# Where a chunk's output lies, in which order its loads are issued, and when two sets of weights are split

## The chip, the cores and the metric

The kernel runs on one core of a Trainium2 chip. Its engines work from queues of their own: TensorE (PE in the rows, PEld for its weight loads), VectorE (DVE), ScalarE (ACT), GpSimd (POOL) and SyncE (SP), which issues nearly all transfers. The metric is the device time of one execution in microseconds. Each engine takes its instructions strictly in the order of its queue, so an instruction that waits holds up all that stand behind it on that engine.

## The reference

One decoder layer on 1024 tokens of width 1024, all in f32. What matters here, cut:

```python
proj = jnp.einsum('bld,de->ble', h, w_in[i])
xs, z, bm, cm, dt_raw, glu, cgate = jnp.split(proj, SPLITS, axis=-1)
...
y = ssd_chunked(xh, dt, a, bm_c, cm_c)          # chunks of 128 tokens
y = y + d_skip * xh
yz = y * jax.nn.silu(z)
yz = yz * lax.rsqrt(jnp.mean(jnp.square(yz), axis=-1, keepdims=True) + RMS_EPS)
y_ssm = yz * ssm_norm_g[i]
...                                             # conformer group: y_conf
mix = jnp.concatenate([y_ssm, y_conf], axis=-1)
out = jnp.einsum('ble,ed->bld', mix, w_out[i]) + b_out[i]
h = layer_norm(DEEPNORM_ALPHA * h + out, ln1_g[i], ln1_b[i])
gate = jax.nn.sigmoid(jnp.einsum('bld,de->ble', h, w_ple_gate[i]))
ple = jnp.einsum('blq,qd->bld', p[i], w_ple_proj[i])
h = layer_norm(DEEPNORM_ALPHA * h + gate * ple, ln2_g[i], ln2_b[i])
```

## The kernel before, in words

Every large matrix product is made of three matmuls of rounded parts: an operand is split into an upper part (a cast on ScalarE) and a lower part (what is left, a subtraction on GpSimd or VectorE), by `split` (L128) or, for weights with a scale, in `out_weight` (L430). `out_weight` loads one slab of 128 rows of weights into `wor` (SP, L433) and leaves `woh` and `wol`.

The work has these stages. First come the embedding norm, the input projection of all 44 column blocks and two causal convolutions; results that later chunks need go to DRAM (`xbc_d`, `z_d`, `acs_d`, `ea_d`, `mix_d`). At about 545 us the last block, a `z_tile`, ends, and its result `zt` is stored to `z_d` (L398).

Then comes the loop over eight chunks of 128 tokens (L698 to L727). Chunk c does on PE, in this order (the order is pinned): `from_state` (L508, `yo`, not for chunk 0), the transposes `xtok` and `bps` of chunk c+1 (`prep`), part of the conformer half of the output projection (`conf_out`, `pso`), `inside` (L521, `yd`), more `pso`, `advance` (L536, `sp`, which moves the state on), `mean_square` of the chunk before (L557, `pr`) and more `pso`. Around it VectorE adds the skip to `yd` and writes the chunk's output `y` (L531); GpSimd multiplies it by silu(z), the tile `sz` that `z_load` brings back from `z_d` (L549); ScalarE squares it into the tile `ea` (L552); GpSimd folds the squares twice (L553, L554); `pr` takes their mean. The loads of chunk c+2 are `prep_load` (`xb` at L454, two `gt` at L459, whose exponentials ScalarE forms at L464), `state_decay` (`ea`, L472) and `z_load` (`sz`, L505). `xb` goes into the place of the chunk two before, which VectorE's `y` reads last.

`y` lives in a pool of two places (tag "y"). Just before the loop the same two places hold `zt` of the last two `z_tile`s and a raw weight tile, and the last `zt` leaves its place when its store has landed.

PE's `yd` and `sp` share three places of PSUM: the second `sp` of a chunk takes that of the first `yd`, which VectorE's `y` has to have read.

After the loop come two products. `out_proj(c)` (L605) multiplies the gated output, read back and split by `y_load` (L590), by the first eight slabs of `wout` (`ws`; slabs 0 to 2 are split inside the loop, 3 to 7 behind it), in four groups `pss` of twelve matmuls, each closed by VectorE's `r` (L616). The groups take turns in two places of PSUM, which `conf_out` uses too: the second group needs the last `ha` (L585) of `conf_out` to have read its place, the third needs the first `r`. In PE's queue the first ten matmuls of group one come first, then ten of group two, then the last two of each (those that read `wol` of slab 3), then groups three and four. `gate` (L630) then multiplies by `wgate` (`wg`, groups `psg`).

A scheduler places instructions on each queue by its own estimate of when each can run. `tc.keep_in_program_order(...)` exempts an instruction from that: it stays where the program has it. The lines that set it in the parts touched:

```python
def on_pe(ins):
    if pinned:
        tc.keep_in_program_order(ins)
...
nc.scalar.activation(out=h.bitcast(F32R), in_=raw, func=AF.Copy, scale=scale)
tc.keep_in_program_order(nc.vector.scalar_tensor_tensor(out=l.bitcast(F32R), ...))
```

Of the kernel before, what the change touches and what calls it, by code (L numbers as in the profile page):

```python
# [9 lines left out]
F32R = mybir.dt.float32r  # L10
AF = mybir.ActivationFunctionType
ALU = mybir.AluOpType
PSUM = bass.MemoryType.PSUM

P = 128
L = 1024
D = 1024
NK = 8
NT = 8
HEADS = 16  # L20
HD = 64
# [25 lines left out]
def tile_block(ctx: ExitStack, tc: tile.TileContext, x, pT, wple, win, wdt, wout, wgate, vec, rows, heads, out):  # L47
    nc = tc.nc
# [24 lines left out]
    z_d = tc.dram_tile([NT, P, NK, P], F32, name="z_d")  # L73
    acs_d = tc.dram_tile([P, P], F32, name="acs_d")
# [6 lines left out]
    def work(name, tag, n=L):  # L81
        return wk.tile([P, SIZE.get(tag, L)], F32, name=name, tag=tag, bufs=BUFS[tag])[:, 0:n]

    def slabs(a, n=NK):
        return a.rearrange("p (k l) -> p k l", k=n)
# [16 lines left out]
    def v(name, i=0, n=1):  # L102
        return vc[:, VEC[name] + i:VEC[name] + i + n]
# [21 lines left out]
    dec = const.tile([P, P], F32, name="dec")  # L125
    cdec = const.tile([P, P], F32, name="cdec")

    def split(src, h, l, leng):  # L128

        nc.scalar.copy(out=h.bitcast(F32R), in_=src)  # L130
        leng.tensor_tensor(out=l.bitcast(F32R), in0=src, in1=h, op=ALU.subtract)  # L131

    def three(ps, lh, ll, rh, rl, first, last):
        mm(ps, lhsT=ll, rhs=rh, start=first, stop=False)
# [22 lines left out]
    def area(name, tag):  # L157
        return regA.tile([P, L], F32, name=name, tag=tag, bufs={"W": 8, "E": 4, "M": 4}[tag])
# [268 lines left out]
    def bslot(name, tag):  # L427
        return regB.tile([P, D], F32, name=name, tag=tag)

    def out_weight(src, get, tag, last, scale=None, leng=nc.gpsimd):  # L430

        raw = area("wor", last) if last == "W" else work("wor", last) if last else get("wor", tag)
        nc.sync.dma_start(out=raw, in_=src)  # L433
        h, l = get("woh", tag), get("wol", tag)
        if scale is None:
            split(raw, h, l, leng)
        else:
            nc.scalar.activation(out=h.bitcast(F32R), in_=raw, func=AF.Copy, scale=scale)
            tc.keep_in_program_order(nc.vector.scalar_tensor_tensor(out=l.bitcast(F32R), in0=raw, scalar=scale, in1=h, op0=ALU.mult, op1=ALU.subtract))
        return h.bitcast(F32R), l.bitcast(F32R)  # L440

# [3 lines left out]
    def col(a, c, h, n=1):  # L445
        return a[:, c * HEADS + h:c * HEADS + h + n]

    def heads3(a):
        return a.rearrange("p (h d) -> p h d", d=HD)

    def prep_load(c):

        xb = slabs(work("xb", "xb", 12 * P), 12)
        nc.sync.dma_start(out=xb, in_=xbc_d[c])  # L454
        gg = []
        for g in range(2):
            gt = slabs(work("gt", "gt"))
            r0 = c * HEADS + g * 8
            nc.sync.dma_start(out=gt, in_=acs_d[r0:r0 + 8, :].unsqueeze(0).broadcast_to([P, 8, P]))  # L459
            gg.append(gt)  # L460

        for h in range(HEADS):
            sl = gg[h // 8][:, h % 8, :]
            nc.scalar.activation(out=sl, in_=sl, func=AF.Exp, bias=col(nacs, c, h))  # L464
        return xb, gg

    def state_decay(c):

        ea = slabs(work("ea", "u") if c == 0 else area("ea", "E"))
        for q in range(2):  # L470
            er = ea_d[c * HEADS:(c + 1) * HEADS, :].rearrange("(t q) l -> q t l", q=2)[q]
            nc.sync.dma_start(out=ea[q * HD:(q + 1) * HD], in_=er.unsqueeze(0).broadcast_to([HD, NK, P]))  # L472
        return ea

    def prep(c, xb, gg):

        def late(ins):

            if c < 2:
                tc.keep_in_program_order(ins)  # L480

        xdt = work("xdt", "xd")
        xt = pair("xtok")
        for t in range(NK):
            transpose(out=xt[:, t * P:(t + 1) * P], in_=xb[:, t, :], identity=ident)
        late(nc.vector.tensor_tensor(out=heads3(xdt), in0=heads3(xt), in1=col(dtok, c, 0, HEADS).unsqueeze(2).broadcast_to([P, HEADS, HD]), op=ALU.mult))
        xdd = (work("xdd", "u") if c == 0 else area("xdd", "E")) if c + 1 < NT else None
        for h in range(HEADS if c + 1 < NT else 0):
            nc.scalar.activation(out=xdd[:, h * HD:(h + 1) * HD], in_=xdt[:, h * HD:(h + 1) * HD], func=AF.Copy, scale=col(dec, c, h))
        bps = bbank("bps")  # L490
        for g in range(2):
            transpose(out=bps[:, g * P:(g + 1) * P], in_=xb[:, 8 + g, :], identity=ident)
            mm(bps[:, (2 + g) * P:(3 + g) * P], lhsT=xb[:, 8 + g, :], rhs=xb[:, 10 + g, :], start=True, stop=True)
        btok = wk.tile([P, 2 * P], F32, name="btok", tag="btok")
        nc.scalar.copy(out=btok, in_=bps[:, 0:2 * P])
        cbm = wk.tile([P, 2, P], F32, name="cbm", tag="cbm", bufs=1)
        late(nc.vector.tensor_tensor(out=cbm, in0=bps[:, 2 * P:4 * P].rearrange("p (g l) -> p g l", g=2),
                                     in1=tri.unsqueeze(1).broadcast_to([P, 2, P]), op=ALU.mult))
        for g in range(2):
            late(nc.vector.scalar_tensor_tensor(out=gg[g], in0=gg[g], scalar=1.0, in1=cbm[:, g:g + 1, :].broadcast_to([P, 8, P]), op0=ALU.min, op1=ALU.mult))  # L500
        return xb, gg, xdt, xdd, btok

    def z_load(c):
        sz = slabs(work("sz", "u") if c else area("sz", "W"))
        nc.sync.dma_start(out=sz, in_=z_d[c])  # L505
        return sz

    def from_state(c, xb, ea):  # L508

        for g in range(2):  # L510
            es = ea[:, g * 4:g * 4 + 4, :]
            yo = bank("yo")
            for t in range(4):
                j = g * 4 + t
                mm(yo[:, t * P:(t + 1) * P], lhsT=state[:, j * P:(j + 1) * P], rhs=xb[:, 10 + g, :], start=True, stop=True)
            nc.vector.tensor_tensor(out=es, in0=slabs(yo, 4), in1=es, op=ALU.mult)
        if c + 1 < NT:
            nc.gpsimd.tensor_tensor(out=heads3(state), in0=heads3(state),
                                    in1=col(cdec, c, 0, HEADS).unsqueeze(2).broadcast_to([P, HEADS, HD]), op=ALU.mult)
# [70 lines left out]
    def y_load(c):  # L590
        raw = slabs(work("yraw", "y"))
        nc.sync.dma_start(out=raw, in_=y_d[c])
        yH = slabs(work("yH", "xd"))

        split(raw, yH, raw, nc.vector if c < 2 else nc.gpsimd)
        return yH.bitcast(F32R), raw.bitcast(F32R)


# [83 lines left out]
    regs = [(bslot, "B1")] * 4 + [(bslot, "B2")] * 4  # L682
    conf = [conf_out(0, *mix_load(0))]
    wc = [out_weight(wout[NK + k], *regs[k], {3: "y", 7: "W"}.get(k)) for k in range(NK)]

    def turn(n):
        for _ in range(n):
            if next(conf[0], conf) is conf:
                conf.pop(0)
                next(conf[0])  # L690

    state = work("state", "st")
    szs = [z_load(0)]
    eas.append(state_decay(1))
    szs.append(z_load(1))
    ws = []
    sq = None
    for c in range(NT):  # L698
        xb, gg, xdt, xdd, btok = ready.pop(0)
        ea = eas.pop(0)  # L700
        y = slabs(work("y", "y"))
        pinned.append(True)
        if c:
            from_state(c, xb, ea)
            if c + 1 < NT:
                ready.append(prep(c + 1, *loaded))
            turn(5)
        for g in range(2):
            inside(c, g, y, xb, gg, ea, xdt)
        turn(3 if c else 2)  # L710
        if c + 1 < NT:
            conf.append(conf_out(c + 1, *mix_load(c + 1)))
        if c:
            turn(2)
        if c + 1 < NT:
            advance(c, xdd, btok)
        if c:
            mean_square(c - 1, sq)
        if c + 2 < NT:
            loaded = prep_load(c + 2)  # L720
            eas.append(state_decay(c + 2))
        sq = gated(c, y, ea, szs.pop(0))
        if c + 2 < NT:
            szs.append(z_load(c + 2))
        if c < 3:
            ws.append(out_weight(wout[c], area, "W", None, v("sng", c)))
        turn(6)  # L727
# [3 lines left out]
    pinned.clear()  # L731
    ys = []
    for k in range(3, NK):
        if k in (4, 6):
            ys.append(y_load(len(ys)))
        ws.append(out_weight(wout[k], area, "W" if k < 4 else "E" if k < 6 else "M", {4: None, 5: "u", 7: "u"}.get(k, "xb"), v("sng", k)))
    gb = []
    for i in range(4):
        r = work(f"gb{i}", "gt")
# [5 lines left out]
    for c in range(2):  # L745
        rs.append(out_proj(c, *ys.pop(0)))
        if c == 0:
            wg = [out_weight(wgate[k], *regs[k], "xb" if k % 4 == 3 else None, leng=nc.vector if k % 2 else nc.gpsimd) for k in range(NK)]
        ys.append(y_load(c + 2))
    for c in range(NT):  # L750
        if c + 2 < NT:
# [57 lines left out]
```

## Time and profile before

| | us |
|---|---|
| median of 3 runs (lowest, highest) | 895.61 (894.19, 896.59) |
| the profiled execution | 894.83 |
| its span | 893.1 |
| PE busy in the span | 863.2 (97%) |
| VectorE, ScalarE, GpSimd busy | 641.2, 389.1, 515.3 |

The span is the part of the execution that the profiler's instructions cover. PE is the engine that works nearly all the time: 29.9 us of the span are left in which it does not. Two stretches stand out in the page's 40 slices, where PE's granted clock shows 8 in place of 9. All times in the rows below count from the start of the span; in brackets stands how long the engine sat idle before a row and what ended that.

### The profile page before, as it was taken

The numbers are of one execution on the slowest core, as the hardware profiler recorded it, in microseconds if no ns is written. First come the engines' busy times: TensorE is split into PE (matmuls) and PEld (weight loads), VectorE is DVE, ScalarE is ACT, GpSimd is POOL, SyncE is SP. The second block draws the span as 40 slices with busy tenths as digits, with TensorE's granted clock in tenths as the row PEclk, the third lists the DMA queues.
The fourth block names the chain that finished last, engine by engine and source line by source line (L and its number), as shares of the span: only waits on it lengthen the run. The fifth ranks groups of instructions, "written<-read, shape, count | busy, mean of one in ns | idle before, by whom it ended". The sixth has DMA issues, their size and how long they took to land. (4 is left out here: it accounts for less than half of the span.)

```text
span 893.1 us, 10971 instructions
## 1 busy us (share of the span) xinstructions
PE 863.2 (97%) x4141; PEld 706.9 (79%) x4141; DVE 641.2 (72%) x739; ACT 389.1 (44%) x633; POOL 515.3 (58%) x297
## 2 busy tenths in 40 slices
PE   6989999999999999999999997999999799999996
PEld 4867888888888888888788885888888678888885
DVE  6968993799999989894403941676654796777765
ACT  4632336767333457553475735745453321111110
POOL 2559829999823299999572254766775362222111
PEclk9999999999999999999999998999999899999999
DMA  9702423121322314233241678799868812222212
GB/s 338 275 36 96 172 87 117 32 95 47 95 67 76 95 47 150 86 95 94 71 141 48 181 245 273 265 345 294 262 222 295 310 42 95 95 94 77 83 51 74
DMA packets 67716, 126.42 MB, mean 142 GB/s; under 512 B 4176, under 2 KB 41552, under 8 KB 67664
## 3 DMA queue, kind: packets, MB, share of 16 engines
q1 hardware_dynamic: 67664, 125.73, 42.1%
q8 instruction: 32, 0.52, 0.2%
q14 instruction: 20, 0.16, 0.1%
HBM read 89.93 MB, written 35.78 MB: 141 GB/s over the span
## 5 line engine op out<-in xcount | busy, mean ns | idle before, releaser
L57 PE MATMUL ps<-hL,wh 128*128 128x512 f32 x704 | 274.6, 391 | 1.1 <-DVE hL L190 1.1
L57 PE MATMUL ps<-hH,wl 128*128 128x512 f32 x704 | 274.2, 391 | 1.5 <-DVE hH L188 1.5
L57 PE MATMUL ps<-hH,wh 128*128 128x512 f32 x704 | 274.3, 390 | 0.0
L302 DVE SCALAR_TENSOR_TENSOR pc<-u,vc,pc 128x1024 f32<-128x1024 f32 x174 | 223.9, 1287 | 3.5
L297 POOL TENSOR_TENSOR acc<-acc,prod 128x1024 f32<-128x1024 f32 x60 | 146.4, 2440 | 17.9 <-ACT acc L293 15.0
L131 POOL TENSOR_TENSOR wl<-wraw,wh 128x1024 fp32r<-128x1024 f32 x44 | 110.7, 2515 | 77.1 <-PE ps L57 41.4
L57 PEld LDWEIGHTS ps<-hL,wh 128*128 128x128 f32 x704 | 132.2, 188 | 29.0 <-DVE hL L190 1.5
L57 PEld LDWEIGHTS ps<-hH,wl 128*128 128x128 f32 x704 | 131.8, 188 | 28.8 <-DVE hH L188 2.0
L57 PEld LDWEIGHTS ps<-hH,wh 128*128 128x128 f32 x704 | 132.2, 188 | 27.5 <-issue 0.2
L143 POOL TENSOR_SCALAR ve<-mv 128x1 f32<-128x1 f32 x23 | 15.8, 688 | 142.3 <-DVE mv L154 100.0
L296 ACT ACTIVATE prod<-u,vc 128x1024 f32<-128x1024 f32 x60 | 69.0, 1153 | 45.7 <-POOL acc L297 35.6
L130 ACT CAST wh<-wraw 128x1024 fp32r<-128x1024 f32 x44 | 46.2, 1051 | 67.0 <-DMA wraw<-in_win_dram 40.7
L643 ACT ACTIVATE gt<-psg 128x512 f32<-128x512 f32 (+1 forms) x17 | 9.7, 573 | 120.4 <-PE psg L57 120.4
L391 DVE SCALAR_TENSOR_TENSOR pc<-xin,vc,pc 128x512 f32<-128x512 f32 x72 | 53.7, 750 | 6.0 <-ACT pc L258 3.4
L57 PE MATMUL pss<-woh,yraw 128*128 128x512 f32 x128 | 51.3, 402 | 5.7 <-DVE r L616 5.7
L57 PE MATMUL pso<-woh,mL 128*128 128x512 f32 x128 | 53.6, 419 | 0.0
L57 PE MATMUL psg<-woh,hTL 128*128 128x512 f32 (+1 forms) x136 | 52.0, 383 | 0.0
L57 PE MATMUL psg<-woh,hTH 128*128 128x512 f32 (+1 forms) x136 | 52.0, 382 | 0.0
L616 DVE SCALAR_TENSOR_TENSOR r<-pss,rsm,r 128x512 f32<-128x512 f32 x32 | 23.8, 747 | 39.2 <-PE pss L57 32.7
L57 PE MATMUL psg<-wol,hTH 128*128 128x512 f32 (+1 forms) x136 | 51.5, 378 | 0.0
L57 PE MATMUL pss<-woh,yH 128*128 128x512 f32 x128 | 50.6, 396 | 0.0
L57 PE MATMUL pso<-wol,mH 128*128 128x512 f32 x128 | 50.6, 395 | 0.0
(184 smaller groups left out, 1460.7 us busy)
## 6 DMA issues: line engine op xcount, KB each, us to landing
wraw<-in_win_dram SPq DMA_DIRECT2D x44, 512.0 KB, 3.6
gt<-acs_d SPq DMA_DIRECT2D x16, 512.0 KB, 4.6
wor<-in_wout_dram SPq DMA_DIRECT2D x16, 512.0 KB, 5.6
xbc_d<-cacc SPq DMA_DIRECT2D x12, 512.0 KB, 3.4
xb<-xbc_d SPq DMA_DIRECT2D x8, 768.0 KB, 6.6
xt<-in_x_dram SPq DMA_DIRECT2D x8, 512.0 KB, 9.0
ple_d<-pl SPq DMA_DIRECT2D x8, 512.0 KB, 4.8
ha_d<-xt SPq DMA_DIRECT2D x8, 512.0 KB, 4.8
```

Of the source, the lines that this page charges most:

```text
L57: on_pe(nc.tensor.matmul(*args, **kw))
L130: nc.scalar.copy(out=h.bitcast(F32R), in_=src)
L131: leng.tensor_tensor(out=l.bitcast(F32R), in0=src, in1=h, op=ALU.subtract)
L143: eng.tensor_scalar(out=ve, in0=var, scalar1=EPS, scalar2=None, op0=ALU.add)
L296: nc.scalar.activation(out=pr, in_=u[:, i:i + L], func=AF.Copy, scale=v("ccw", j * KC + i))
L297: nc.gpsimd.tensor_tensor(out=acc, in0=acc, in1=pr, op=ALU.add)
L302: nc.vector.scalar_tensor_tensor(out=pc if i + 1 < KC else acc, in0=u[:, i:i + L], scalar=v("ccw", j * KC + i), in1=pc, op0=ALU.mult, op1= ...
L391: nc.vector.scalar_tensor_tensor(out=pc, in0=xin[:, o + j:o + j + 512], scalar=v("scw", i * 4 + j), in1=pc, op0=ALU.mult, op1=ALU.add)
L616: nc.vector.scalar_tensor_tensor(out=r[:, nn], in0=ps, scalar=rss[c][:, g:g + 1], in1=r[:, nn], op0=ALU.mult, op1=ALU.add)
L643: nc.scalar.activation(out=gt[:, nn], in_=ps, func=AF.Sigmoid)
```

## The change

The first chunk's `y` is put into the area "W" (the places of the input projection's `hH`, free after its last matmul). The loads of the loop's start are put in another order, and those of chunk 2 and the first `sz` are pinned in it (`behind`). Chunk 1's gated output is loaded and split behind all eight slabs of `wout`, its lower part on GpSimd in place of VectorE and pinned. The upper parts of scaled weights are pinned as well, and both parts of the gate weights.

```diff
@@ -125,10 +125,13 @@
     dec = const.tile([P, P], F32, name="dec")
     cdec = const.tile([P, P], F32, name="cdec")
 
-    def split(src, h, l, leng):
-
-        nc.scalar.copy(out=h.bitcast(F32R), in_=src)
-        leng.tensor_tensor(out=l.bitcast(F32R), in0=src, in1=h, op=ALU.subtract)
+    def split(src, h, l, leng, placed=False):
+
+        upper = nc.scalar.copy(out=h.bitcast(F32R), in_=src)
+        lower = leng.tensor_tensor(out=l.bitcast(F32R), in0=src, in1=h, op=ALU.subtract)
+        if placed:
+            tc.keep_in_program_order(upper)
+            tc.keep_in_program_order(lower)
 
     def three(ps, lh, ll, rh, rl, first, last):
         mm(ps, lhsT=ll, rhs=rh, start=first, stop=False)
@@ -427,15 +430,15 @@
     def bslot(name, tag):
         return regB.tile([P, D], F32, name=name, tag=tag)
 
-    def out_weight(src, get, tag, last, scale=None, leng=nc.gpsimd):
+    def out_weight(src, get, tag, last, scale=None, leng=nc.gpsimd, placed=False):
 
         raw = area("wor", last) if last == "W" else work("wor", last) if last else get("wor", tag)
         nc.sync.dma_start(out=raw, in_=src)
         h, l = get("woh", tag), get("wol", tag)
         if scale is None:
-            split(raw, h, l, leng)
+            split(raw, h, l, leng, placed)
         else:
-            nc.scalar.activation(out=h.bitcast(F32R), in_=raw, func=AF.Copy, scale=scale)
+            tc.keep_in_program_order(nc.scalar.activation(out=h.bitcast(F32R), in_=raw, func=AF.Copy, scale=scale))
             tc.keep_in_program_order(nc.vector.scalar_tensor_tensor(out=l.bitcast(F32R), in0=raw, scalar=scale, in1=h, op0=ALU.mult, op1=ALU.subtract))
         return h.bitcast(F32R), l.bitcast(F32R)
 
@@ -447,6 +450,10 @@
 
     def heads3(a):
         return a.rearrange("p (h d) -> p h d", d=HD)
+
+    def behind(here, ins):
+        if here:
+            tc.keep_in_program_order(ins)
 
     def prep_load(c):
 
@@ -456,7 +463,7 @@
         for g in range(2):
             gt = slabs(work("gt", "gt"))
             r0 = c * HEADS + g * 8
-            nc.sync.dma_start(out=gt, in_=acs_d[r0:r0 + 8, :].unsqueeze(0).broadcast_to([P, 8, P]))
+            behind(c == 2, nc.sync.dma_start(out=gt, in_=acs_d[r0:r0 + 8, :].unsqueeze(0).broadcast_to([P, 8, P])))
             gg.append(gt)
 
         for h in range(HEADS):
@@ -469,7 +476,7 @@
         ea = slabs(work("ea", "u") if c == 0 else area("ea", "E"))
         for q in range(2):
             er = ea_d[c * HEADS:(c + 1) * HEADS, :].rearrange("(t q) l -> q t l", q=2)[q]
-            nc.sync.dma_start(out=ea[q * HD:(q + 1) * HD], in_=er.unsqueeze(0).broadcast_to([HD, NK, P]))
+            behind(c == 2, nc.sync.dma_start(out=ea[q * HD:(q + 1) * HD], in_=er.unsqueeze(0).broadcast_to([HD, NK, P])))
         return ea
 
     def prep(c, xb, gg):
@@ -502,7 +509,7 @@
 
     def z_load(c):
         sz = slabs(work("sz", "u") if c else area("sz", "W"))
-        nc.sync.dma_start(out=sz, in_=z_d[c])
+        behind(c == 0, nc.sync.dma_start(out=sz, in_=z_d[c]))
         return sz
 
     def from_state(c, xb, ea):
@@ -592,7 +599,7 @@
         nc.sync.dma_start(out=raw, in_=y_d[c])
         yH = slabs(work("yH", "xd"))
 
-        split(raw, yH, raw, nc.vector if c < 2 else nc.gpsimd)
+        split(raw, yH, raw, nc.gpsimd if c else nc.vector, c == 1)
         return yH.bitcast(F32R), raw.bitcast(F32R)
 
 
@@ -690,15 +697,14 @@
                 next(conf[0])
 
     state = work("state", "st")
-    szs = [z_load(0)]
     eas.append(state_decay(1))
-    szs.append(z_load(1))
+    szs = []
     ws = []
     sq = None
     for c in range(NT):
         xb, gg, xdt, xdd, btok = ready.pop(0)
         ea = eas.pop(0)
-        y = slabs(work("y", "y"))
+        y = slabs(work("y", "y") if c else area("y", "W"))
         pinned.append(True)
         if c:
             from_state(c, xb, ea)
@@ -718,6 +724,8 @@
             mean_square(c - 1, sq)
         if c + 2 < NT:
             loaded = prep_load(c + 2)
+            if c == 0:
+                szs.extend((z_load(0), z_load(1)))
             eas.append(state_decay(c + 2))
         sq = gated(c, y, ea, szs.pop(0))
         if c + 2 < NT:
@@ -731,9 +739,10 @@
     pinned.clear()
     ys = []
     for k in range(3, NK):
-        if k in (4, 6):
-            ys.append(y_load(len(ys)))
+        if k == 4:
+            ys.append(y_load(0))
         ws.append(out_weight(wout[k], area, "W" if k < 4 else "E" if k < 6 else "M", {4: None, 5: "u", 7: "u"}.get(k, "xb"), v("sng", k)))
+    ys.append(y_load(1))
     gb = []
     for i in range(4):
         r = work(f"gb{i}", "gt")
@@ -745,7 +754,7 @@
     for c in range(2):
         rs.append(out_proj(c, *ys.pop(0)))
         if c == 0:
-            wg = [out_weight(wgate[k], *regs[k], "xb" if k % 4 == 3 else None, leng=nc.vector if k % 2 else nc.gpsimd) for k in range(NK)]
+            wg = [out_weight(wgate[k], *regs[k], "xb" if k % 4 == 3 else None, leng=nc.vector if k % 2 else nc.gpsimd, placed=True) for k in range(NK)]
         ys.append(y_load(c + 2))
     for c in range(NT):
         if c + 2 < NT:
```

The calls of the scheduler lead to these orders. SP's queue at the start of the loop, before (`ea_4188`, `gt_4243`, `xb_4241`: decays of chunk 1, loads of chunk 2; `z_d_98` from `zt_4069` is the last `z_tile`'s store; `sz_4186` and `sz_4191` belong to chunks 0 and 1):

```order
L472 DMA ea_4188<-ea_d_100 64x8x128 x2
L472 DMA ea_4263<-ea_d_100 64x8x128 x2
L398 DMA z_d_98<-zt_4069 128x8x128
L459 DMA gt_4243<-acs_d_99 128x1024
L459 DMA gt_4245<-acs_d_99 128x1024
L505 DMA sz_4186<-z_d_98 128x1024
L570 DMA mraw_4227<-mix_d_96 128x1024
L433 DMA wor_4273<-in_wout_dram 128x1024
L454 DMA xb_4241<-xbc_d_97 128x1536
L505 DMA sz_4191<-z_d_98 128x1024
L550 DMA y_d0_88<-y_4193 128x1024
```

and now:

```order
L479 DMA ea_4186<-ea_d_100 64x8x128 x2
L401 DMA z_d_98<-zt_4069 128x8x128
L577 DMA mraw_4223<-mix_d_96 128x1024
L461 DMA xb_4237<-xbc_d_97 128x1536
L466 DMA gt_4239<-acs_d_99 128x1024
L466 DMA gt_4241<-acs_d_99 128x1024
L512 DMA sz_4259<-z_d_98 128x1024
L512 DMA sz_4261<-z_d_98 128x1024
L479 DMA ea_4263<-ea_d_100 64x8x128 x2
L436 DMA wor_4273<-in_wout_dram 128x1024
L557 DMA y_d0_88<-y_4189 128x1024
```

`xb` of chunk 2 stood behind two `gt`, an `sz`, a `mraw` and a `wor` and now stands ahead of all but `mraw`; the second pair of `ea` moved from ahead of the `z_d` store to behind both `sz`.

ScalarE's queue at the same place, before (`gt_...` the exponentials of chunk 2, `ea_3270` the square of chunk 0's output, `xdd_4323` of chunk 2):

```order
L130 CAST woh_4181<-wor_4179 128x1024
L464 ACT_TABLE_LOAD
L464 ACTIVATE gt_4243<-gt_4243,nacs_122 128x128 x8
L464 ACTIVATE gt_4245<-gt_4245,nacs_122 128x128 x8
L130 CAST mH_4231<-mraw_4227 128x1024
L552 ACTIVATE ea_3270<-y_4193 128x1024
L438 ACTIVATE woh_4275<-wor_4273,vc_101 128x1024
L495 COPY btok_4345<-bps_4340 128x256
L489 ACTIVATE xdd_4323<-xdt_4312,dec_123 128x64 x16
```

and now:

```order
L130 CAST woh_4181<-wor_4179 128x1024
L130 CAST mH_4227<-mraw_4223 128x1024
L471 ACT_TABLE_LOAD
L471 ACTIVATE gt_4239<-gt_4239,nacs_122 128x128 x8
L471 ACTIVATE gt_4241<-gt_4241,nacs_122 128x128 x8
L502 COPY btok_4345<-bps_4340 128x256
L496 ACTIVATE xdd_4323<-xdt_4312,dec_123 128x64 x16
L559 ACTIVATE ea_3270<-y_4189 128x1024
L441 ACTIVATE woh_4275<-wor_4273,vc_101 128x1024
```

The square of chunk 0 stood ahead of `btok` and `xdd` and now stands behind them.

VectorE's queue at the end of the loop, before (`wol_5542`, `5548`, `5559`, `5565`, `5531` are slabs 4, 5, 6, 7 and 3; `yraw_5551` is the lower part of chunk 1's gated output; `r_5576` of chunk 0):

```order
L131 TENSOR_TENSOR yraw_5534<-yraw_5534,yH_5536 128x1024
L439 SCALAR_TENSOR_TENSOR wol_5542<-wor_5539,vc_101,woh_5541 128x1024
L585 TENSOR_TENSOR ha_5338<-ha_5338,pso_5456 128x512
L564 TENSOR_SCALAR vem_5517<-pr_5513 128x2
L439 SCALAR_TENSOR_TENSOR wol_5548<-wor_5545,vc_101,woh_5547 128x1024
L585 TENSOR_TENSOR ha_5338<-ha_5338,pso_5494 128x512
L439 SCALAR_TENSOR_TENSOR wol_5531<-wor_5528,vc_101,woh_5530 128x1024
L131 TENSOR_TENSOR yraw_5551<-yraw_5551,yH_5553 128x1024
L439 SCALAR_TENSOR_TENSOR wol_5559<-wor_5556,vc_101,woh_5558 128x1024
L439 SCALAR_TENSOR_TENSOR wol_5565<-wor_5562,vc_101,woh_5564 128x1024
L616 SCALAR_TENSOR_TENSOR r_5576<-pss_5578,rsm0_4430,r_5576 128x512
```

and now (slabs 6 and 7 are `wol_5554` and `5560`):

```order
L131 TENSOR_TENSOR yraw_5534<-yraw_5534,yH_5536 128x1024
L442 SCALAR_TENSOR_TENSOR wol_5542<-wor_5539,vc_101,woh_5541 128x1024
L592 TENSOR_TENSOR ha_5338<-ha_5338,pso_5456 128x512
L571 TENSOR_SCALAR vem_5517<-pr_5513 128x2
L442 SCALAR_TENSOR_TENSOR wol_5548<-wor_5545,vc_101,woh_5547 128x1024
L442 SCALAR_TENSOR_TENSOR wol_5554<-wor_5551,vc_101,woh_5553 128x1024
L442 SCALAR_TENSOR_TENSOR wol_5560<-wor_5557,vc_101,woh_5559 128x1024
L592 TENSOR_TENSOR ha_5338<-ha_5338,pso_5494 128x512
L442 SCALAR_TENSOR_TENSOR wol_5531<-wor_5528,vc_101,woh_5530 128x1024
L623 SCALAR_TENSOR_TENSOR r_5576<-pss_5578,rsm0_4430,r_5576 128x512
```

The `yraw` of chunk 1 is gone from this queue; slabs 6 and 7 went from behind the last `ha` to ahead of it. On GpSimd chunk 1's `yraw` now stands right behind the last `rsm`, and the first gate weight's lower part behind chunk 0's norm.

## Rows read from the trace of the kernel before

**Rows 1.** The view by windows of one us, PE only: time, busy, granted clock, DMA share, GB/s
```profile
551.00:552.00 1.00, 0.00 (x0) 0.75 1.04 418
```

**Rows 2.** The timeline of PE, first chunk: start us, length us, engine, line, operation, tiles
```profile
547.08 1.02 PE L57 MATMUL sp<-xdd,btok 128*128 128x512 f32 x2
...
553.15 2.05 PE L57 MATMUL sp<-xdd,btok 128*128 128x512 f32 x2 [5.04 <-DVE y L531]
...
560.66 1.95 PE L57 MATMUL yo<-xb,state 128*128 128x128 f32 x16
```

**Rows 3.** The timeline of SP's queue and VectorE, first chunk
```profile
544.92 0.64 SPq L398 DMA_DIRECT2D z_d<-zt  x1
...
551.88 2.15 DVE L531 SCALAR_TENSOR_TENSOR y<-xb,vc,yd 128x128 f32<-128x128 f32 x8 [15.84 <-DMA z_d<-zt]
```

**Rows 4.** The timeline of PE, second chunk
```profile
562.44 1.04 PE L60 MATMUL xtok<-ident,xb 128*128 128x128 f32 x8
...
572.94 1.88 PE L57 MATMUL sp<-xdd,btok 128*128 128x512 f32 x4
...
574.65 0.50 PE L57 MATMUL pr<-inv,ea 128*128 128x1 f32 x4
...
579.19 1.95 PE L57 MATMUL yo<-xb,state 128*128 128x128 f32 x16
```

**Rows 5.** The DMA issues from 538 to 566 us: count, KB each, median us to landing
```profile
gt<-acs_d SPq DMA_DIRECT2D x2, 512.0 KB, 6.8
...
wor<-in_wout_dram SPq DMA_DIRECT2D x4, 512.0 KB, 5.4
...
xb<-xbc_d SPq DMA_DIRECT2D x1, 768.0 KB, 6.3
```

**Rows 6.** The timeline of ScalarE, first and second chunk
```profile
553.03 1.28 ACT L464 ACT_TABLE_LOAD   x1 [6.90 <-DMA gt<-acs_d]
...
554.33 4.78 ACT L464 ACTIVATE gt<-gt,nacs 128x128 f32<-128x128 f32 x16
...
559.96 1.05 ACT L552 ACTIVATE ea<-y 128x1024 f32<-128x1024 f32 x1
...
566.84 3.94 ACT L489 ACTIVATE xdd<-xdt,dec 128x64 f32<-128x64 f32 x16 [2.29 <-DVE xdt L486]
```

**Rows 7.** The timeline of GpSimd, second chunk
```profile
564.55 2.27 POOL L553 TENSOR_TENSOR ea<-ea 128x512 f32<-128x512 f32 x1
...
566.90 0.75 POOL L554 TENSOR_TENSOR ea<-ea 128x256 f32<-128x256 f32 x1
...
570.97 1.29 POOL L534 TENSOR_TENSOR y<-y,ea 128x512 f32<-128x512 f32 x1 [3.33 <-DVE y L531]
```

**Rows 8.** The timeline of VectorE, end of the chunk loop
```profile
691.89 1.28 DVE L439 SCALAR_TENSOR_TENSOR wol<-wor,vc,woh 128x1024 fp32r<-128x1024 f32 x1
...
693.29 0.69 DVE L585 TENSOR_TENSOR ha<-ha,pso 128x512 f32<-128x512 f32 x1
...
696.99 2.01 DVE L131 TENSOR_TENSOR yraw<-yraw,yH 128x1024 fp32r<-128x1024 f32 x1 [1.82 <-ACT yH L130]
...
698.92 4.55 DVE L439 SCALAR_TENSOR_TENSOR wol<-wor,vc,woh 128x1024 fp32r<-128x1024 f32 x2
...
703.39 1.40 DVE L616 SCALAR_TENSOR_TENSOR r<-pss,rsm,r 128x512 f32<-128x512 f32 x2
```

**Rows 9.** The timeline of PE, first output projection
```profile
693.09 0.40 PE L57 MATMUL pss<-woh,yraw 128*128 128x512 f32 x1
...
704.19 0.80 PE L57 MATMUL pss<-woh,yraw 128*128 128x512 f32 x1 [5.48 <-DVE r L616]
...
708.58 0.39 PE L57 MATMUL pss<-wol,yH 128*128 128x512 f32 x1
```

**Rows 10.** The timeline of SP's queue and GpSimd, end of the chunk loop
```profile
684.90 0.49 SPq L433 DMA_DIRECT2D wor<-in_wout_dram  x1
...
699.02 3.37 POOL L131 TENSOR_TENSOR wol<-wor,woh 128x1024 fp32r<-128x1024 f32 x1 [1.11 <-ACT woh L130]
```

## The prediction

> **What bounds the kernel now.** I read the page's totals first: PE is busy 863.2 of 893.1 us, so what the change is worth is decided by the 29.9 us in which PE stands. Two gaps make 10.5 of them; the other 19 lie nearly all ahead of PE's first matmul and behind its last, which no edit touches. The timeline of PE finds them. The first stands before the second `sp` of the first chunk: 5.04 us, released by VectorE's `y` [rows 2]. The second stands before the third group of the first output projection: 5.48 us, released by VectorE's `r` [rows 9]. The windows show what else a gap costs: in its fourth microsecond PE's granted clock is 0.75 in the mean, so it fell to its lower level, 1.2 GHz, within it [rows 1], and the matmul after the second gap takes 0.80 where it takes 0.40 before it and 0.39 later [rows 9].
>
> Then I looked at what the releasers wait for. `y` waited 15.84 us for the store of `zt`, issued at 544.92 and landed by 551.88 [rows 3]: the two places of tag "y" are both held by `zt`, and the product that `y` reads was ready. `r` waited for no data: it stood in VectorE's queue behind `yraw` of chunk 1 (2.01, after 1.82 of waiting for ScalarE) and two `wol` that took 4.55 [rows 8].
>
> **First gap.** With a place in "W" `y` has nothing left to wait for but its operands, and the second `sp` follows the first as it does in the next chunk. There the stretch from `sp` to the next `yo` takes 579.19 − 572.94 = 6.25, less some 0.45 for the four `pr` that the first chunk doesn't have: 5.8 [rows 4]. So `yo` starts at 547.08 + 5.8 = 552.9 and not at 560.66 [rows 2]: 7.8 us, the 5.04 of the wait and 2.7 of the lower clock.
>
> What is late next? First `xb` of chunk 2: it takes the place that `y` of the first chunk reads last, so it is issued at about 547.5, and 6.3 later [rows 5] is at 553.8. `xtok` needs it 562.44 − 560.66 = 1.78 after `yo` [rows 2, 4], at 554.7; 0.9 us are left. Loading it ahead of `gt` and `sz` is what makes this fit.
>
> Second, `pr` of the first chunk, which PE reaches 574.65 − 560.66 = 13.99 after `yo` [rows 2, 4], at 566.9. Its input takes a chain. `gt` is issued behind `xb`, at about 548, and lands 6.8 later [rows 5], at 554.8; table load 1.28 and exponentials 4.78 bring ScalarE to 560.8 [rows 6]. Now come the chunk's `xdd`, 3.94, which the new order puts ahead of the square: 564.8. Square 1.05: 565.9 [rows 6]. GpSimd's folds take 2.27 (the slower value) and 0.75, and an addition of 1.29 may stand between them [rows 7]: 569.2 to 570.2. PE would wait 2.3 to 3.3 there; if `gt` lands 1.5 earlier, since the two transfers of `ea` that stood ahead now stand behind, 0.8. I take 2.4, near the end that the rows give. Before, the square came at 559.96, ahead of `xdd` at 566.84 [rows 6], and `pr` never waited. The gap's net gain is 7.8 − 2.4 = 5.4. Its bounds are 7.8 (no wait) and about 0.3: a wait of 5 and the clock lost with it.
>
> A rule of the Trainium skill speaks against this term: by "SBUF — State Buffer", section "Who interferes with whom", a VectorE instruction with two inputs in SBUF and a GpSimd instruction that reads SBUF shut each other out for the length of a whole instruction. The rows agree in kind: `wol` takes 1.28 alone [rows 8], and two take 4.55 while GpSimd's own `wol` takes 3.37 [rows 8, 10]. By that rule the `wol` of slab 0 on VectorE could hold up each fold by up to 1.28, and the wait for `pr` would be about 3.7 in place of 2.4. That alone would make the sum 885.3; it also leads to the first rival, whose price and chance below come from rows.
>
> **Second gap.** In the new order `vem`, `wol` of slabs 5, 6 and 7, the last `ha` and `wol` of slab 3 stand ahead of `r`, without a `yraw`. From 691.89, three `wol` of 1.28 end at 695.7 and `ha` of 0.69 at 696.4 [rows 8]. PE begins group one at 693.09 [rows 9]. A matmul of this kind comes every 0.23 at the full clock: eighteen `pso` make up 4.1 us of the stretch from `pr` to `yo`, which is 4.54 [rows 4]. Its first ten end at 695.4, and the next ten need the last `ha`: PE waits 1.1, a wait that this edit adds, since before, `ha` ended at 693.98. Its ten end at 698.7 and the two left of group one at 699.35. Then `r` runs, half of 1.40 [rows 8], and group three starts at 700.1, and not at 704.19 [rows 9]: 4.1 us. The ten matmuls from there to 708.58 take 4.39 now [rows 9] and 2.3 at the full clock: 2.1 more. Together 6.2.
>
> Behind the late `ha` only `wol` of slab 3 is queued, needed at 698.7, and `r`. The load of slab 7 was issued at 684.90 [rows 10] and lands 5.4 later [rows 5], at 690.3, with its cast by about 692, before VectorE comes to it at 694.5. Chunk 1's `yraw` on GpSimd, behind the last `rsm`, costs 2.0 to 3.4 there [rows 8, 10] and ends near 701 at the latest; its product begins twelve matmuls times two behind the third group's start, 5.5 later, at 705.6. So it is covered by 4. Bounds of this term: 0, if the time is lost again behind it, and 6.6, if GpSimd's absence makes `wol` quick and nothing else waits.
>
> What now waits longer are the gate weights. Two raw loads of them stand behind `yraw` of chunk 2 in SP's queue (its place comes free when PE ends the first product, near 705) and two more behind that of chunk 3 (the end of the second, near 717.5). At 5.4 a load [rows 5] and some 3 for the split [rows 10] the last are there by 726, and `gate` needs them from about 728. I cost that at nothing, with 2 us of cover.
>
> **The other edits.** The pinned upper parts and ScalarE's and GpSimd's order in chunks 2 and 3 I cost at nothing: PE waits for nothing between 553.15 and the second gap. The square's cover is the 14 us to `pr`; in later chunks it has its old place. VectorE's `wol` of slabs 1 and 2 now stand ahead of a chunk's own tiles; that is the last rival.
>
> **Sum.** The profiled execution took 894.83: 894.83 − 5.4 − 6.2 = 883.2. The median of the runs stands 0.8 above the profiled one, so 884.0.
>
> **Rivals.** (A) The wait for `pr` reaches the length at which the clock falls. In both gaps it had fallen by the fourth microsecond [rows 1]; so from about 3.6 us the wait costs itself and 2.7 more, 6.5 in all, and the first gap gives 1.3: 888. For it: my chain comes to 3.3 without any delay, and folds beside VectorE's `wol` may be slower. Against: `gt` may land earlier with fewer transfers ahead of it. 0.14.
>
> (B) The second gap is given back at `gate`: the split weights come some 4 us late, since SP's queue holds four of their loads behind `yraw`. The tail then gives nothing: 894.83 − 5.4 + 0.8 = 890.2. For it: 2 us of cover on estimates each uncertain by as much. Against: the needs come one slab after another, and half of the splits lie on an engine that is free. 0.11.
>
> (C) Slower. `wol` of slab 1 stands on VectorE ahead of the second chunk's decay products, of `y` and so of all that PE takes from them, and its load has moved behind others in SP's queue. If `wor` lands late, VectorE stands with that whole queue behind it, and PE waits 5 us and loses 2.7 with the clock, as in the first gap [rows 2], in each of the two chunks that split such a slab: 15.4 against the 11.6 of the forecast, so 884.0 + 15.4 = 899.4. It decides from a landing after about 577, when PE is at the next `yo` (579.19 before [rows 4], some 5 earlier now). For it: a queue in strict order is what made both gaps. Against: loads land in 5.4 [rows 5] and there are some 10 us. 0.06.
>
> (D) The new place in "W" is still held, by a reader of the input projection's last tile or by another tile of that tag, and `y` waits as before: only the second gap's 6.2 is gained, 889.4. Against: the last matmul that reads `hH` lies before `zt`'s end. 0.03.
>
> (E) Gains and new waits cancel, and nothing is seen: 895.6. 0.04.
>
> **Chances.** The forecast holds 0.62. A, B and D make it faster too: 0.90 in all. No change is 0.04 and slower 0.06; I count as change more than 0.3%, 2.7 us, about what a measurement of this kernel can tell from none. The likeliest case's own range goes from 881 (the wait for `pr` 0.8, and 1.4 more from a quicker VectorE) to 887.6 (a wait of 3.3, and 2.7 of the second gap lost). For 8 in 10 I go on to 890.6, which takes in A, D and B, and down to 880.8.
>
> **What would show it.** Right: in the first chunk `y` starts at about 545 and the second `sp` has no idle time before it; granted clock 1.00 through 550 to 560; `yo` near 553; a wait of PE before the second chunk's `pr` of 0.8 to 3.3, ended by GpSimd's fold. At the projection one wait of about 1.1 before group two, ended by `ha`, and none of over 3 before group three, with matmuls of 0.39 there; no idle time at `gate`. The forecast is wrong if `pr` waits over 3.6 and the clock falls behind it, if `xtok` waits for `xb`, if PE waits at `gate` for a weight, or if a wait ended by VectorE's `wol` stands in the second or third chunk.

## The result, and the profile after

The changed kernel takes 889.92 us (median of 4 runs, 889.28 to 891.57) beside 895.97 of the kernel before on the same chip. By the medians that is 6.1 us less, where 11.6 were forecast; the ratio estimated from all the runs is 0.9939, 95% interval 0.9918 to 0.9959. The time lies outside the likeliest case's own range (881 to 887.6) and within the wider one, 0.7 from its slow end (890.6); the size is wrong. The profiled execution has a span of 887.4, 5.7 less than before. PE is busy 862.1 of it, VectorE 640.3, ScalarE 389.7, GpSimd 517.6: nearly the same work. PE stands for 25.3 us (887.4 − 862.1) and not for 29.9, so 4.6 of the 5.7 are waits.

The first chunk, PE's timeline (start, length, engine, line, operation, tiles, and in brackets the idle time and what ended it); it answers to [rows 2, 4]:

```profile
545.37 1.97 PE L57 MATMUL yd<-gt,xdt 128*64 128x128 f32 x32
...
548.76 1.88 PE L57 MATMUL sp<-xdd,btok 128*128 128x512 f32 x4
...
554.61 1.95 PE L57 MATMUL yo<-xb,state 128*128 128x128 f32 x16
...
572.14 0.70 PE L57 MATMUL pr<-inv,ea 128*128 128x1 f32 x4 [3.38 <-POOL ea L561]
...
573.28 0.63 PE L57 MATMUL pso<-wol,mH 128*128 128x512 f32 x1
...
578.41 1.95 PE L57 MATMUL yo<-xb,state 128*128 128x128 f32 x16
```

The four `sp` run in one piece: the wait for `y` of [rows 2] is gone. In its place stands a wait of 3.38 before `pr`, ended by GpSimd's second fold, and behind it matmuls take 0.63 in place of 0.39. The windows of one us (busy, granted clock, DMA share, GB/s) show the clock there; before, PE waited for nothing in this stretch:

```profile
570.00:571.00 1.00, 0.00 (x0) 1.00 0.97 377
...
572.00:573.00 1.00, 0.86 (x5) 0.76 1.02 369
573.00:574.00 1.00, 1.00 (x3) 0.50 1.01 410
...
575.00:576.00 1.00, 1.00 (x4) 0.53 1.04 238
576.00:577.00 1.00, 1.00 (x6) 1.00 0.79 274
```

The end of the loop and the projections, PE; it answers to [rows 9]:

```profile
695.44 0.50 PE L57 MATMUL pss<-woh,yraw 128*128 128x512 f32 x1 [0.69 <-DVE ha L592]
...
699.34 0.50 PE L57 MATMUL pss<-woh,yraw 128*128 128x512 f32 x1 [0.39 <-DVE r L623]
...
701.78 0.39 PE L57 MATMUL pss<-wol,yH 128*128 128x512 f32 x1
...
732.13 0.51 PE L57 MATMUL pss<-woh,yraw 128*128 128x512 f32 x1 [1.43 <-DVE r L623]
```

The 5.48 before group three is 0.39, group two waits 0.69 for the late `ha` (1.1 were forecast), and the matmuls behind are at the full clock. New is the last row: 1.43 before the last group of the product of chunk 2.

From one mark to the next (the first `yd` of the loop stands at 543.69 in the trace before) the two profiled executions compare so:

| stretch | before | after | gain | forecast |
|---|---|---|---|---|
| start of the span to first `yd` | 543.69 | 545.37 | −1.68 | 0 |
| first `yd` to first `yo` | 16.97 | 9.24 | 7.73 | 7.8 |
| first `yo` to second `yo` | 18.53 | 23.80 | −5.27 | −2.4 |
| second `yo` to third group `pss` | 125.00 | 120.93 | 4.07 | 4.1 |
| third group to the end of the span | 188.91 | 188.06 | 0.85 | 2.1 |
| sum | 893.1 | 887.4 | 5.70 | 11.6 |

All instructions ahead of the first `yd` stand in the same order in both kernels, but for the second pair of `ea`, which SP issues there in the kernel before alone; the mark's time is taken up under the experiments. From the first `yd` on the two executions differ by 7.4 (349.4 and 342.0 to the end of the span), so it is in part luck that the 5.70 of the table lies near the 6.1 of the medians.

### The profile page after: what moved, and what is told of

It is laid out like the page before. It is cut to its first block, busy times and chain, and to the rows that moved or that the text cites. A ratio compares the mean times of both kernels' runs of the same rounds, so it can differ in the third digit from the quotient of the medians.

```text
span 887.4 us, 10975 instructions
## 1 busy us (share of the span) xinstructions
PE 862.1 (97%) x4141; PEld 704.8 (79%) x4141; DVE 640.3 (72%) x738; ACT 389.7 (44%) x633; POOL 517.6 (58%) x298
## 4 chain that ended last, share of the span: by engine, by line
PE 86%; DVE 6%; issue 2%; DMA 2%; ACT 1%; POOL 1%; SPq 0%; DVEq 0%; POOLq 0%; ACTq 0%
PE ps L57 54%; PE psg L57 9%; PE pss L57 7%; PE pso L57 7%; PE yd L57 1%; PE yo L57 1%; DVE st L155 1%; PE sp L57 1%; DMA gt<-acs_d 1%; DMA wor<-in_wout_dram 1%; DMA ppraw<-in_pT_dram 1%; DVE hH L191 1%; PE pt L60 1%; PE xtok L60 1%; PE psp L57 1%
## 5 line engine op out<-in xcount | busy, mean ns | idle before, releaser
L146 POOL TENSOR_SCALAR ve<-mv 128x1 f32<-128x1 f32 x23 | 19.1, 831 | 134.5 <-DVE mv L157 89.3
L57 PE MATMUL pso<-woh,mH 128*128 128x512 f32 x128 | 50.4, 394 | 0.0
```

The source lines that it names most:

```text
L57: on_pe(nc.tensor.matmul(*args, **kw))
L146: eng.tensor_scalar(out=ve, in0=var, scalar1=EPS, scalar2=None, op0=ALU.add)
```

## The experiments

**The place alone.** The kernel before with one line changed; every engine's order stays as it was.

```diff
-        y = slabs(work("y", "y"))
+        y = slabs(work("y", "y") if c else area("y", "W"))
```

> The kernel before with one line changed: the first chunk's y in area W; every engine's order is that of before. Theory: y starts about 545 and the second sp follows the first, but sz of chunk 0 stands in SP's queue ahead of mraw, wor and xb of chunk 2 and waits for the z_d store (landed 551.88 before), so xb is issued near 552.5 and lands near 559. xtok of chunk 2 needs it at 554.7: PE waits about 4 us there and the clock falls, so of 7.7 only 0 to 2 are kept: 894 to 896. Rival (the order of the loads buys nothing, the square stands ahead of xdd as before, so nothing new waits): all 7.7 are kept, about 888.

Measured: 896.00 against 895.22 (ratio 1.0009, 0.9991 to 1.0027). Nothing is left of the gain. The `sp` doesn't wait (first `yd` to first `yo` 9.23), but the next thing in the chunk does. SP's queue, and PE:

```profile
547.77 0.38 SPq L398 DMA_DIRECT2D z_d<-zt  x1
...
554.69 0.32 SPq L505 DMA_DIRECT2D sz<-z_d  x1
...
556.06 0.38 SPq L454 DMA_DIRECT2D xb<-xbc_d  x1
```

```profile
555.72 1.95 PE L57 MATMUL yo<-xb,state 128*128 128x128 f32 x16
563.85 1.97 PE L60 MATMUL xtok<-ident,xb 128*128 128x128 f32 x8 [6.19 <-DMA xb<-xbc_d]
...
582.55 1.95 PE L57 MATMUL yo<-xb,state 128*128 128x128 f32 x16
```

`sz` can't be issued before the store of `zt` has landed, 6.9 after its issue, and `xb` stands behind it. From `yo` to `yo` it takes 26.83 and not 18.53: 6.19 of waiting and 2.1 of the lower clock. So the order of the loads is what makes the place worth anything; the rival, that it buys nothing, is out.

**The start alone.** The changed kernel with the tail's edits taken back.

```diff
-        split(raw, yH, raw, nc.gpsimd if c else nc.vector, c == 1)
+        split(raw, yH, raw, nc.vector if c < 2 else nc.gpsimd)
...
-        if k == 4:
-            ys.append(y_load(0))
+        if k in (4, 6):
+            ys.append(y_load(len(ys)))
...
-    ys.append(y_load(1))
...
-            wg = [... leng=nc.vector if k % 2 else nc.gpsimd, placed=True) ...]
+            wg = [... leng=nc.vector if k % 2 else nc.gpsimd) ...]
```

> The changed kernel with the tail of before (places of y_load, splits, gate weights not pinned). Theory: the start of the loop gives what the trace of after shows there, 7.7 less the 5.3 between the first and the second yo (wait for pr 3.4, 1.7 of lower clock, 0.2 else): 2.4, so 893.5; the wait for pr stands at 3.0 to 3.6. Rival (the start is worth the forecast 5.4 and the median hides it by other losses): 890.5.

Measured: 892.85 against 895.22 (0.9970, 0.9950 to 0.9991), 2.4 less. The forecast 5.4 is not there. Its profile:

```profile
569.62 0.61 PE L57 MATMUL pr<-inv,ea 128*128 128x1 f32 x4 [3.06 <-POOL ea L561]
...
571.10 0.56 PE L57 MATMUL pso<-wol,mH 128*128 128x512 f32 x1
...
575.90 1.95 PE L57 MATMUL yo<-xb,state 128*128 128x128 f32 x16
...
697.70 0.80 PE L57 MATMUL pss<-woh,yraw 128*128 128x512 f32 x1 [2.27 <-DVE r L623]
```

The tail isn't quite that of before: one `wol` now stands behind `r` (the upper parts are still pinned), and group three waits 2.27 and not 5.48. So the median is a mixture, and that it came out at the expected 2.4 confirms little: the twelve runs go from 887.72 to 897.07, the profiled one took 888.58, and from the first `yd` to the end of the span it takes 5.9 less than before (343.5 and 349.4). By the marks, the first `yd` (543.16) to the second `yo` takes 32.74 here, 35.50 before and 33.04 after: the start is worth 2.5 to 2.8.

**The tail alone.** The changed kernel with `y` in its old place and the loads in their old order.

```diff
-        if here:
+        if False:
...
+    szs = [z_load(0)]
     eas.append(state_decay(1))
-    szs = []
+    szs.append(z_load(1))
...
-        y = slabs(work("y", "y") if c else area("y", "W"))
+        y = slabs(work("y", "y"))
...
-            if c == 0:
-                szs.extend((z_load(0), z_load(1)))
```

> The changed kernel with the start of before (y in its old place, loads in the old order). Theory: the tail gives 6.2 at groups two to four of the first product, less 1.2 to 1.4 at the last group of chunk 2's product, where VectorE's r comes late: 4.9, so 891.0; the wait of 5.0 before the second sp stands as before. Rival (the start gave the forecast 5.4, and the tail what is left of 6.0): 895.3.

Measured: 891.83 against 895.22 (0.9956, 0.9938 to 0.9974), 3.4 less, between the two expectations and nearer the first. Its profile has the old wait before the second `sp`:

```profile
552.31 2.04 PE L57 MATMUL sp<-xdd,btok 128*128 128x512 f32 x2 [5.39 <-DVE y L538]
```

It has none at the last group of chunk 2's product, where 1.4 was expected: from the second `yo` (578.16) to the span's end (886.3) takes 308.14, where after takes 308.99 and before 313.91. So by the marks the tail gains 5.8, and by the medians 3.4; the profiled execution (888.0) is the fastest of the seven, and what the others lose isn't known. By the medians start and tail add up to 5.8, and the whole was measured at 6.1; with part of the tail's gain in both of them this shows little.

**The square ahead of `xdd`.** ScalarE's order changed in the changed kernel; with it, on GpSimd, both folds come ahead of both additions.

```diff
-            nc.scalar.activation(out=xdd[...], ..., func=AF.Copy, scale=col(dec, c, h))
+            behind(c == 2, nc.scalar.activation(out=xdd[...], ..., func=AF.Copy, scale=col(dec, c, h)))
...
-        nc.scalar.activation(out=sq, ..., func=AF.Square)
+        behind(c == 0, nc.scalar.activation(out=sq, ..., func=AF.Square))
```

> The changed kernel with the square of chunk 0 and the sixteen xdd of chunk 2 kept in the program's order, so that the square stands ahead of xdd on ScalarE (and GpSimd's two folds ahead of both additions). Theory (the square behind xdd makes pr late; xdd is needed only a chunk later): square near 563, folds done by 566, pr at 568.8 doesn't wait, clock 1.00 from 566 to 580: 5 us less than after, about 885; up to 1 us may come back at xtok of chunk 3, whose load now stands behind others. Rival (ScalarE's whole chain is late from gt on, and what is put behind the square waits in its place): about 889 to 890, with a new PE wait in the third chunk.

Measured: 884.95 against 895.22 (0.9885, 0.9867 to 0.9902). That is 10.3 less than before, where the changed kernel was 6.1 less beside its own runs of before: 4.2 us more, or 5.0 by its median of 889.92. ScalarE and PE:

```profile
561.40 1.05 ACT L559 ACTIVATE ea<-y 128x1024 f32<-128x1024 f32 x1
...
564.27 3.92 ACT L496 ACTIVATE xdd<-xdt,dec 128x64 f32<-128x64 f32 x16
```

```profile
554.20 1.95 PE L57 MATMUL yo<-xb,state 128*128 128x128 f32 x16
...
568.20 0.50 PE L57 MATMUL pr<-inv,ea 128*128 128x1 f32 x4
...
572.74 1.95 PE L57 MATMUL yo<-xb,state 128*128 128x128 f32 x16
576.48 1.09 PE L60 MATMUL xtok<-ident,xb 128*128 128x128 f32 x8 [1.80 <-DMA xb<-xbc_d]
```

`pr` doesn't wait, and no matmul behind it is slow. What came back is 1.80 at `xtok` of chunk 3, more than the 1 us that was expected at most, behind which the clock stays at full speed, and 0.40 at a later `xtok`. From the first `yd` to the end of the span it takes 339.2 and the changed kernel 342.0: by the marks the order is worth 2.8, less than by the medians.

**Again, and the norm ahead of chunk 3's lower part.** The changed kernel unedited, and with one more split pinned:

```diff
-        split(raw, yH, raw, nc.gpsimd if c else nc.vector, c == 1)
+        split(raw, yH, raw, nc.gpsimd if c else nc.vector, c in (1, 3))
```

> The changed kernel once more, nothing edited, for the spread. Theory (the first yd of the loop starts anywhere from 542.5 to 546.5 with the same instructions ahead of it, so single profiles differ by that): median 889 to 890.5; the wait for pr 3.0 to 3.6 with matmuls of 0.63 behind it, from first to second yo 23.3 to 24.0, the wait at the last group of chunk 2's product 1.2 to 1.5. Rival (the later start of 545.37 belongs to the change): the first yd again at 545 or later, in every profile of kernels with this start, and not in those without it.

> The changed kernel with the lower part of chunk 3's gated output kept in the program's order on GpSimd, so that ve and rs of chunk 1's norm come ahead of it. Theory (VectorE's scaled r of chunk 1 waits for that rs, and r of chunk 2 stands behind it): rs 2 us earlier, the wait of 1.43 at the last group of chunk 2's product falls to 0.3 or less, 1.2 us in all: 888.7. Rival (VectorE is full there, its 3.4 and 3.5 us norm instructions set r, wherever rs ends): the wait stays at 1.0 or more, 889.9.

Measured against 896.61: 887.61 again (0.9910, 0.9879 to 0.9940) and 887.56 pinned (0.9909, 0.9882 to 0.9936). The runs of this chip spread more (883.5 to 891.6 of the one kernel), and the two medians can't be told apart; what the pin does is seen in the traces alone.

```profile
572.98 0.61 PE L57 MATMUL pr<-inv,ea 128*128 128x1 f32 x4 [3.60 <-POOL ea L561]
```

Both waits are there again as expected, this one and 1.41 at the last group of chunk 2's product; the median is below the expected 889 to 890.5.

GpSimd and VectorE in the changed kernel, then with the pin:

```profile
722.90 2.41 POOL L131 TENSOR_TENSOR yraw<-yraw,yH 128x1024 fp32r<-128x1024 f32 x1 [2.53 <-ACT yH L130]
725.29 1.19 POOL L146 TENSOR_SCALAR ve<-mv 128x1 f32<-128x1 f32 x1
726.56 1.41 POOL L148 TENSOR_TENSOR rs<-ve,mhalf 128x1 f32<-128x1 f32 x1
```

```profile
722.86 3.54 DVE L607 SCALAR_TENSOR_TENSOR r<-r,mv,gb 128x1024 f32<-128x1024 f32 x1
...
728.00 3.42 DVE L610 SCALAR_TENSOR_TENSOR r<-r,rs,gb 128x1024 f32<-128x1024 f32 x1 [0.47 <-POOL rs L148]
731.34 1.40 DVE L623 SCALAR_TENSOR_TENSOR r<-pss,rsm,r 128x512 f32<-128x512 f32 x2
```

```profile
721.28 1.31 POOL L146 TENSOR_SCALAR ve<-mv 128x1 f32<-128x1 f32 x1 [2.54 <-DVE mv L157]
722.68 1.41 POOL L148 TENSOR_TENSOR rs<-ve,mhalf 128x1 f32<-128x1 f32 x1
724.06 2.39 POOL L131 TENSOR_TENSOR yraw<-yraw,yH 128x1024 fp32r<-128x1024 f32 x1
```

```profile
721.23 1.28 DVE L607 SCALAR_TENSOR_TENSOR r<-r,mv,gb 128x1024 f32<-128x1024 f32 x1
...
724.12 3.41 DVE L610 SCALAR_TENSOR_TENSOR r<-r,rs,gb 128x1024 f32<-128x1024 f32 x1 [0.47 <-POOL rs L148]
727.45 1.40 DVE L623 SCALAR_TENSOR_TENSOR r<-pss,rsm,r 128x512 f32<-128x512 f32 x2
```

With the pin PE has no wait there, and from its third group

```profile
697.74 0.50 PE L57 MATMUL pss<-woh,yraw 128*128 128x512 f32 x1 [0.39 <-DVE r L623]
```

to the end of the span (884.1) it takes 186.36, where after and again take 188.06 and 188.00: 1.7 less. The same pin on top of the square's new order takes this stretch from 187.9 to 186.3.

**Both, and the slabs later.** The square first and the pin together; then also slabs 0 to 2 of `wout` one chunk later:

```diff
-        if c < 3:
-            ws.append(out_weight(wout[c], area, "W", None, v("sng", c)))
+        if 0 < c < 4:
+            ws.append(out_weight(wout[c - 1], area, "W", None, v("sng", c - 1)))
```

> sq_first and y3_pinned together. Theory: their gains add, 884.95 less 1.2: 883.7, with the wait of 1.8 at xtok of chunk 3 as in sq_first. Rival (the rest of the tail's time is set by VectorE): 885.

> The kernel before this one with slabs 0 to 2 of wout loaded and split one chunk later (chunks 1 to 3), so that no wol stands between the two halves of the second chunk's y and no wor transfer ahead of xb of chunk 3. Theory (xb waits for the end of y, and y was split by wol, which waits for its load): y of chunk 1 ends 1.2 earlier, xb is issued at about 567.5 relative to a first yd at 545 and lands by 574.5, the wait of 1.8 at xtok of chunk 3 falls to 0.5 or less: 1.3 to 2 less, 881.7 to 882.4. Rival (the transfer is slow, 7.7, as the queues are full at 0.99 of their time): the wait stays over 1.2, 883.5, or comes back in chunk 4 with the later slab.

Measured against 896.61: 883.00 (0.9857, 0.9832 to 0.9883) and 882.48 (0.9856, 0.9829 to 0.9883). They are 4.6 and 5.1 below the changed kernel's 887.61, measured beside the same runs of before; the two can't be told apart. The wait at `xtok` of chunk 3 (1.28 in the first) is gone in the second, and three others stand in its place, 2.2 together:

```profile
568.24 1.10 PE L57 MATMUL sp<-xdd,btok 128*128 128x512 f32 x2 [0.35 <-DVE y L538]
...
594.75 1.09 PE L60 MATMUL xtok<-ident,xb 128*128 128x128 f32 x8 [0.55 <-DMA xb<-xbc_d]
...
607.67 1.10 PE L57 MATMUL sp<-xdd,btok 128*128 128x512 f32 x2 [1.34 <-DVE y L538]
```

The longest stands in the fourth chunk, ended by a `y` that has a slab's `wol` ahead of it on VectorE (602.29 to 603.67). So the loss moved to a later chunk, as the rival had it, and from the first `yd` to the end of the span takes 337.9, against 336.9 with the slabs in their old place.

**The start of the span.** The first `yd` stands at 543.69, 545.37, 546.49 (the place alone), 543.16 (the start alone), 542.50 (the tail alone), 544.97, 545.99 (again), 543.14, 545.48 and 545.36, with the same instructions ahead of it but for the pair of `ea`. The latest has the place alone and the earliest the tail alone, and the changed kernel's own are 545.37 and 545.99 where its variants with the same start have 543.14 to 545.48: the 1.68 of the table is within the spread, and nothing ties it to the change.

## Why the prediction was wrong, and where it was right

**The wait for `y`: right.** 7.73 of 7.8; `y` waits for `yd` alone now, where it waited for the store in [rows 3]. VectorE, first and second chunk:

```profile
546.51 2.16 DVE L538 SCALAR_TENSOR_TENSOR y<-xb,vc,yd 128x128 f32<-128x128 f32 x8 [8.79 <-PE yd L57]
...
568.58 1.69 DVE L442 SCALAR_TENSOR_TENSOR wol<-wor,vc,woh 128x1024 fp32r<-128x1024 f32 x1 [0.94 <-ACT woh L441]
```

**`xb` in time: right.** `xtok` follows `yo` without a wait, and the place without the order of the loads gave nothing.

**The wait for `pr`: the step that failed.** The prediction put it at "2.3 to 3.3" and went on: "I take 2.4, near the end that the rows give". ScalarE's and GpSimd's rows answer to [rows 6, 7]:

```profile
562.62 3.94 ACT L496 ACTIVATE xdd<-xdt,dec 128x64 f32<-128x64 f32 x16
566.46 1.04 ACT L559 ACTIVATE ea<-y 128x1024 f32<-128x1024 f32 x1
```

```profile
566.67 1.29 POOL L541 TENSOR_TENSOR y<-y,ea 128x512 f32<-128x512 f32 x1 [5.23 <-DVE y L538]
567.92 1.26 POOL L560 TENSOR_TENSOR ea<-ea 128x512 f32<-128x512 f32 x1
569.14 2.25 POOL L541 TENSOR_TENSOR y<-y,ea 128x512 f32<-128x512 f32 x1
571.36 0.73 POOL L561 TENSOR_TENSOR ea<-ea 128x256 f32<-128x256 f32 x1
```

ScalarE's part came out: `xdd` was to end 21.1 after the first `yd` (564.8 − 543.69) and did 21.2 after it (566.56 − 545.37). But on GpSimd both additions to the second chunk's `y` got ahead of the second fold, not one that "may stand between". The first addition had waited for VectorE's `y` and ended at 567.96, 0.46 after the square, so the first fold stood behind it and not behind the square. The second addition took 2.25 in place of 1.29, while VectorE's `wol` ran (568.58 to 570.27). The first fold's 1.26, where the prediction had charged 2.27, gave 1.0 back. So the folds ended 26.7 after the first `yd` (572.09 − 545.37), where the prediction's chain gives 25.5 to 26.5, and PE waited 3.38, in the other profiles with this order 3.06, 3.57 and 3.60: the late end of the rows' span or beyond it, where 2.4 had been taken from the early end. An estimate from these rows: with both additions behind the folds, these would have ended at 569.5 (567.50 + 1.26 + 0.73), and PE, which came at 568.76, would have waited 0.7. GpSimd's order made most of the wait. By the rule of the Trainium skill that the prediction weighed ("SBUF — State Buffer", section "Who interferes with whom") the wait was 3.7; the four waits, 3.4 in the mean, lie nearer to it than to 2.4, though what was held up was an addition and not a fold.

**The clock behind it: the larger part of the miss.** The prediction let the clock fall only "from about 3.6 us". It fell behind waits of 3.38 (0.50 in the windows from 573 on) and of 3.06. From `pr` to `yo` takes 6.27 (578.41 − 572.14) where it took 4.54 [rows 4]: 1.7. The wait and the clock are 5.1 of the 5.27 that the stretch lost, and the first gap gave 7.73 − 5.27 = 2.5, not 5.4. That is rival (A), to which I gave 0.14, with 2.5 where it had 1.3. The numbers of (D) and (B), 889.4 and 890.2, lie closer to the 889.92 measured, but neither of their mechanisms is in the traces. [rows 1] told me of one clock in one long wait, and I read a boundary out of it. The windows of the trace before speak against 3.6 already: PE stood from 548.11 in the first gap, and the 0.75 of [rows 1] puts the fall at 551.5, 3.4 later; in the second gap it stood from 698.71, and the 0.84 of this window puts the fall at 701.7, 3.0 later.

```profile
701.00:702.00 1.00, 0.00 (x0) 0.84 1.06 434
```

That the orders of the two queues caused the wait and the clock is shown by a run: with the square ahead of `xdd` on ScalarE, and the folds ahead of the additions on GpSimd, `yo` to `yo` takes 18.54 (572.74 less 554.20 in its trace) as it did before. No run turned only one of the two.

**The second gap: right.** Three `wol` stand ahead of `ha` on VectorE (it answers to [rows 8]):

```profile
691.11 3.68 DVE L442 SCALAR_TENSOR_TENSOR wol<-wor,vc,woh 128x1024 fp32r<-128x1024 f32 x3
```

PE's wait for `ha` is the 0.69 above; the start of the third group gains 4.07 of 4.1, and the ten matmuls behind it take 2.44 (701.78 − 699.34), not 4.39 [rows 9]: 1.95 of 2.1.

**"I cost that at nothing": wrong by 1.2.** I looked for the gate weights behind `yraw` on SP, and they came in time; rival (B) didn't happen. It was the norm. `yraw` of chunk 3 got ahead of the norm's `ve` and `rs` on GpSimd, VectorE's last norm instruction waited for `rs`, and `r`, which PE's last group needs, stood behind it. That the wait was absent in the run of the tail alone, in the same order, suggests how narrow it is (one profile): there the cast of chunk 3's output began 3.8 after its load's issue (720.66 − 716.89), in the changed kernel 5.2 (721.77 − 716.54). The pinned split took it away.

**Not seen:** (C), a wait for `wol` in the second or third chunk, and (D), since `y` didn't wait.

## What to carry to other kernels

When a wait goes away, the work behind it comes earlier, and what was comfortably ready is not: follow each later operand of that engine back through its queues, with every instruction that the new order lets in between, and take those at the price that they have beside others, not alone. Where rows give a span for such a wait, take the late end, and add what the slower clock costs behind it: here a wait of 3.4 cost 5.1. An operation that is needed next belongs ahead of one that is needed a chunk later; here that order was worth another 4.2 to 5.0 us by the medians, and 2.8 by the marks.

## What the hardware showed that was not expected

- The clock fell to half with waits of 3.06, 3.38, and, in the run of the start alone, 2.27 (the matmul behind it took 0.80), but not with 1.80 at `xtok` of chunk 3. With the wait of 3.06 PE had been back at work at the full clock for 1.5 us (569.62 to 571.10) when its matmuls became slow; with the wait of 2.27 the clock fell while PE still stood. The cost was 1.7 with 3.06 and 3.38, and 2.1 with 6.19.
- A VectorE instruction that reads two tiles of SBUF took 3.54 beside a GpSimd `yraw` of 2.41 and 1.28 without it (the first rows of VectorE in the two traces of the norm): 2.26 longer, nearly the whole of the other's instruction.
- The same instructions up to the first `yd` (but for one pair of loads) took 542.50 to 546.49 in ten profiled executions. Single profiles of this kernel differ by up to 4 us there, and are compared mark by mark.
